# First block of a fused two-block transformer kernel: GpSimd arithmetic moved to VectorE and ScalarE, and the memory input split 512 columns at a time

## The chip, the cores and the metric

The kernel runs on one core of one Trainium2 chip. The metric is the device time of one execution in microseconds; lower is better. The core's engines work side by side, each through its own queue in order: TensorE (PE in the rows, PEld for its weight loads), VectorE (DVE), ScalarE (ACT), GpSimd (POOL) and SyncE (SP), which issues the DMAs. Engines wait for one another by semaphores.

## The reference, cut to what matters

256 tokens of width 1024 pass through a first block (depth 1) and a second one (two layers). The change is in the first part of the first block and in a softmax helper that all attentions share.

```python
# first_block, one layer
xn = rmsnorm(h, norm_mix_g[l])
proj = xn @ w_in[l]
q, k, v, u, y = jnp.split(proj, [...], axis=-1)          # 512 columns each
q = rope(q...); k = rope(k...)                            # 8 heads of 64
attn = dilated_mixture_attention(q, k, v)
uc = centred_depthwise_conv(u, conv_w[l], conv_b[l])      # 4 taps
rec = bidirectional_rglru(uc, ...) * jax.nn.gelu(y)
h = h + jnp.concatenate([attn, rec], axis=-1) @ w_out[l]
h = h + memory_cross_attention(rmsnorm(h, ...), rmsnorm(memf, norm_mem_g[l]), ...)
hid = jnp.square(jax.nn.relu(rmsnorm(h, ...) @ w_mlp_in[l]))
h = h + hid @ w_mlp_out[l]

# bidirectional_rglru
r = sigmoid(gate_a(u)); i = sigmoid(gate_x(u))
log_a = -RG_C * r * softplus(-lam)
a = exp(log_a)
b = sqrt(-expm1(2.0 * log_a)) * (i * u)
h_f = scan(a[0], b[0]);  h_b = reverse scan(a[1], b[1]);  return h_f + h_b
```

## The kernel before

Activations are kept with features on the 128 partitions and the 256 tokens along the free dimension. Every weight comes from one stream `W` in blocks of 8 tiles of 128x128, in the order in which they are used. A block is copied in by SyncE (`w`), rounded to a high part by ScalarE (`whi`, line 366) and its remainder taken as a low part (`wlo`, line 368): on VectorE, but on GpSimd for the blocks 6, 9, 12, 15 and 18 (`POOL`). A product of a weight tile with an activation tile is then three matmuls: high by high, high by low, low by high (lines 392 to 394, or 633 to 635 where the weights are the moving side). There are four buffers each of `whi` and `wlo`, so the split of block n waits until TensorE is done with block n-4. I number blocks from 0: u has 0 to 3, q 4 to 7, k 8 to 11, v 12 to 15, y 16 to 19, the memory keys 20 to 23, the output projection 24 to 31. The matmuls of these products (`pl`) I call filler, since small work of the mixers is put between them.

Around them run, as generators: `rglru` (conv `uc`, gates `tr` and `ti`, `e` the exponential, `s` the square root, scans, sum of the two directions), `attention` (8 heads; each head has scores `sc`, maximum on VectorE, exponential `p` on ScalarE, scaling by `rd` in `times`, transposes `ptp`, their copy `pts`, product with the values `po`), `mem_prep` (squares and split of the memory input into `mh` and `ml`), and the rotary products in `c_rope`. `times` is also used by the cross attention and, in the second block's layers, by the two softmax mixers `diff` and `mla`.

The order on each engine is not the order of the code: the build places instructions by a model of their times, with priorities that `urgent` and `norm_later` raise. What stands in that order is therefore a fixed fact of each program.

Of the kernel before, what the change touches and what calls it, by code (L numbers as in the profile page):

```python
# [9 lines left out]
F32 = mybir.dt.float32  # L10
# [4 lines left out]
AF = mybir.ActivationFunctionType  # L15
# [12 lines left out]
NL, NX = 3, 4  # L28
NW = 5
SB = 8  # L30
POOL = range(6, 20, 3)
WARM = 36
G4, H2 = 16, 12
A0, A1 = 2, 4
# [249 lines left out]
class Kern:  # L284
# [71 lines left out]
    def _split(self):  # L356
        t0, size = self.parts[self.ns]
        b, o = divmod(t0, TB)
        while self.nd < min(b + self.depth, self.nblk):
            self._dma()  # L360
        w = self.blk_dma[b][:, o * 128:(o + size) * 128]
        if o + size == TB:
            self.blk_dma.pop(b)
        hi = self.wp.tile([128, SB * 128], F32R, name="whi", tag="whi", bufs=4)[:, :size * 128]
        lo = self.wp.tile([128, SB * 128], F32R, name="wlo", tag="wlo", bufs=4)[:, :size * 128]
        self.nc.scalar.activation(hi, w, AF.Copy)  # L366
        eng = self.nc.gpsimd if t0 // TB in POOL else self.nc.vector
        eng.tensor_tensor(lo, w, hi.bitcast(F32), op=OP.subtract)  # L368
        self.blk_split[self.ns] = (hi, lo)
        self.ns += 1  # L370

# [151 lines left out]
class Body(Kern):  # L523
# [166 lines left out]

    def times(self, p, r):

        self.nc.gpsimd.tensor_tensor(p, p, r.rearrange("p (q o) -> p q o", o=1).to_broadcast([128, 2, T]),  # L693
                                     op=OP.mult)

    def transpose_p(self, p):

# [23 lines left out]
    def setup(self):  # L721
        nc, a, cst = self.nc, self.a, self.cst
        self.h = cst.tile([128, KD, T], F32, name="h")
        self.pt = cst.tile([128, a["P"].shape[1]], F32, name="pt")
        self.ct = cst.tile([128, a["C"].shape[1]], F32, name="ct")
        self.mk = cst.tile([128, 896], U8, name="mk")
        self.xx = cst.tile([128, KD, 2, T], F32R, name="xx")
        self.xh, self.xl = self.xx[:, :, 0], self.xx[:, :, 1]

        z = cst.tile([128, 128], BF16, name="warm")  # L730
        nc.vector.memset(z, 0.0)
        wp = self.psl("warm")
        for _ in range(WARM):
            nc.tensor.matmul(wp[:, :128], z, z, start=True, stop=True)

        nc.scalar.activation(self.small("first", 1), z[:, :1], AF.Square)
        nc.sync.dma_start(self.pt, a["P"])
        for _ in range(32 // TB):
            self._dma()
        self.pos = cst.tile([128, 64], I32, name="pos")  # L740
        p = a["pos"]
        nc.gpsimd.dma_start(self.pos, bass.AP(tensor=p.tensor, offset=p.offset, ap=[[64, 4], [0, 32], [1, 64]]))
        nc.sync.dma_start(self.ct, a["C"])
        self.mhalf = cst.tile([128, 16], F32, name="mhalf")
        nc.gpsimd.memset(self.mhalf, -0.5)

    def setup_late(self):
        nc, a, cst = self.nc, self.a, self.cst
# [178 lines left out]
    def block1(self):  # L927
# [15 lines left out]
        rm = {}  # L943

        def mem_prep():
            nm = Norm(self)
            for j in range(4):
                m = self.mem[j // 2]
                o = 2 * (j % 2)
                sq = self.square(m[:, o:o + 2])  # L950
                for c in range(2):
                    k = 2 * j + c
                    self.split(mh[k // 4][:, k % 4], ml[k // 4][:, k % 4], m[:, k % 4],
                               scale=self.G("norm_mem_g")[:, k:k + 1])
                yield
                nm.add(sq)
            yield
            rm["r"] = self.rpow("mr", nm.sums(), 2, 1.0 / D, EPS)
            yield
            rm["b"] = nm.spread(rm["r"], "mb")  # L960
            yield
# [10 lines left out]
        def c_rope(dst):  # L972
            def f(k, ps, n):
                qe = self.h2("qe")
                V.tensor_tensor(qe, ps, self.bT(r1["b"]), op=OP.mult)
                sw = self.swap(qe, 32)

                def later():
                    V.tensor_tensor(qe, qe, self.bT(self.rope[:, 0]), op=OP.mult)
                    nc.gpsimd.tensor_tensor(sw, sw, self.bT(self.rope[:, 1]), op=OP.mult)  # L980
                    V.tensor_tensor(dst[:, k:k + 2], qe, sw, op=OP.add)
                self.defer(later)
            return f
# [4 lines left out]
        def rglru():  # L988
            yield
            cw, cb = self.G("conv_w"), self.G("conv_b")  # L990
            for c in range(4):
                nc.gpsimd.tensor_scalar(uc[:, c], ut[:, c], cw[:, 4 * c + 2:4 * c + 3], cb[:, c:c + 1],
                                        op0=OP.mult, op1=OP.add)
                for k in (0, 1, 3):
                    lo, hi = max(0, 2 - k), T - max(0, k - 2)
                    o = uc[:, c, lo:hi]
                    V.scalar_tensor_tensor(o, ut[:, c, lo + k - 2:hi + k - 2],
                                           cw[:, 4 * c + k:4 * c + k + 1], o, op0=OP.mult, op1=OP.add)
                if c % 2:
                    yield  # L1000
            pre = []
            for z in range(2):
                tr, ti = self.g4("tr"), self.g4("ti")
                for j in range(2):
                    pa = self.ps("pga").rearrange("p (c t) -> p c t", c=2)
                    px = self.ps("pgx").rearrange("p (c t) -> p c t", c=2)
                    for c in range(2):
                        k = 2 * j + c
                        nc.tensor.matmul(pa[:, c], self.gb[0][:, z * 4 + k], uc[:, k], start=True, stop=True)
                        nc.tensor.matmul(px[:, c], self.gb[1][:, z * 4 + k], uc[:, k], start=True, stop=True)  # L1010
                    for c in range(2):
                        k = 2 * j + c
                        i = z * 4 + k
                        nc.scalar.activation(tr[:, k], pa[:, c], AF.Tanh, bias=self.hb[:, i:i + 1], scale=0.5)
                        nc.scalar.activation(ti[:, k], px[:, c], AF.Tanh, bias=self.hb[:, 8 + i:9 + i], scale=0.5)
                    yield

                V.scalar_tensor_tensor(tr, tr, 1.0, self.sp2[:, 4 * z:4 * z + 4].rearrange("p (k o) -> p k o", o=1)
                                       .to_broadcast([128, 4, T]), op0=OP.add, op1=OP.mult)
                s, e = self.g4("s"), self.g4("e")  # L1020
                nc.scalar.activation(e, tr, AF.Exp, scale=-2.0)
                last = nc.scalar.activation(s, tr, AF.Tanh)
                V.scalar_tensor_tensor(ti, ti, 1.0, uc, op0=OP.add, op1=OP.mult)
                yield

                nc.gpsimd.tensor_scalar(e, e, 0.5, 0.5, op0=OP.mult, op1=OP.add)
                V.scalar_tensor_tensor(tr, s, 1.0, e, op0=OP.add, op1=OP.mult)
                V.scalar_tensor_tensor(e, tr, 2.0, e, op0=OP.subtract, op1=OP.mult)
                nc.gpsimd.tensor_tensor(ti, ti, e, op=OP.mult)
                pre.append((tr, ti, s, e))  # L1030
                yield

            with self.tc.issue_after(last.ins):
                for tr, ti, s, e in pre:
                    nc.scalar.activation(s, s, AF.Sqrt)
            yield
            for z, (tr, ti, s, e) in enumerate(pre):
                V.tensor_tensor(ti, ti, s, op=OP.mult)
                nc.gpsimd.tensor_scalar(e, e, -2.0, -1.0, op0=OP.mult, op1=OP.add)
                for k in range(4):  # L1040
                    if z == 0:
                        V.tensor_tensor_scan(tr[:, k], e[:, k], ti[:, k], 0.0, OP.mult, OP.subtract)
                    else:
                        V.tensor_tensor_scan(tr[:, k, ::-1], e[:, k, ::-1], ti[:, k, ::-1], 0.0,
                                             OP.mult, OP.subtract)
                yield
            self.hh = pre[0][0]
            nc.gpsimd.tensor_tensor(self.hh, pre[0][0], pre[1][0], op=OP.add)

        rg = urgent(self.tc, rglru(), HR)  # L1050

# [9 lines left out]
        def c_y(k, ps, n):  # L1061
# [1 line left out]
            y = yt[:, k:k + 2]  # L1063
            V.tensor_tensor(y, ps, self.bT(r1["b"]), op=OP.mult)
            w = self.h2("yw")
            nc.scalar.activation(w, y, AF.Square)
            nc.gpsimd.tensor_scalar(w, w, 0.044715, 1.0, op0=OP.mult, op1=OP.add)
            nc.gpsimd.tensor_tensor(w, w, y, op=OP.mult)
            nc.scalar.activation(w, w, AF.Tanh, scale=math.sqrt(2 / math.pi))
            V.scalar_tensor_tensor(y, w, 1.0, y, op0=OP.add, op1=OP.mult)  # L1070

# [739 lines left out]
```

## Time and profile before

| | |
|---|---|
| median of 3 runs | 1342.47 us (1341.91 to 1343.61) |
| the profiled execution, its own time | 1340.12 us |
| span of its instructions | 1338.3 us |
| mean granted TensorE clock | 0.982 |
| TensorE busy | 95% of the span |
| VectorE, ScalarE, GpSimd busy | 73%, 50%, 19% |

A busy share is an average over stages: most of the span is long matrix products in which TensorE never stops, while the first 137 us are the mixed stage that the change touches. So that stage has to be read by itself, by who waits for whom in it.

### The profile page before, as it was taken

The numbers are of one execution on the slowest core, as the hardware profiler recorded it, in microseconds if no ns is written. First come the engines' busy times: TensorE is split into PE (matmuls) and PEld (weight loads), VectorE is DVE, ScalarE is ACT, GpSimd is POOL, SyncE is SP. The second block draws the span as 40 slices with busy tenths as digits, with TensorE's granted clock in tenths as the row PEclk, the third lists the DMA queues.
The fourth block names the chain that finished last, engine by engine and source line by source line (L and its number), as shares of the span: only waits on it lengthen the run. The fifth ranks groups of instructions, "written<-read, shape, count | busy, mean of one in ns | idle before, by whom it ended". The sixth has DMA issues, their size and how long they took to land. (4 is left out here: it accounts for less than half of the span.)

```text
span 1338.3 us, 21771 instructions
## 1 busy us (share of the span) xinstructions
PE 1277.3 (95%) x8514; PEld 1159.8 (87%) x8514; DVE 974.8 (73%) x1398; ACT 667.4 (50%) x1018; POOL 258.7 (19%) x209
## 2 busy tenths in 40 slices
PE   7969999999989889999999999998899999999998
PEld 7957978888879888899988888898788999888886
DVE  6998548775568997656777776689966667777754
ACT  5556446554444226444555554442363545555542
POOL 8764111000012331222010000024212220100000
PEclk9989999999999999999999999998998999999999
DMA  8532445565564353245555566544431355555552
GB/s 275 172 118 96 141 126 166 190 190 189 194 205 150 118 181 95 89 143 179 179 184 190 189 200 223 168 146 127 159 125 64 129 186 175 179 191 191 191 187 68
DMA packets 68599, 216.45 MB, mean 162 GB/s; under 512 B 10376, under 2 KB 16008, under 8 KB 68496
## 3 DMA queue, kind: packets, MB, share of 16 engines
q1 hardware_dynamic: 68448, 215.02, 49.0%
q8 instruction: 67, 1.10, 0.4%
q14 instruction: 36, 0.29, 0.1%
q0 software_dynamic: 48, 0.03, 0.0%
HBM read 208.73 MB, written 1.05 MB: 157 GB/s over the span
## 5 line engine op out<-in xcount | busy, mean ns | idle before, releaser
L368 DVE TENSOR_TENSOR wlo<-w,whi 128x1024 fp32r<-128x1024 f32 (+1 forms) x381 | 490.0, 1289 | 236.1 <-ACT whi L366 233.7
L366 ACT ACTIVATE whi<-w 128x1024 fp32r<-128x1024 f32 (+1 forms) x386 | 404.2, 1051 | 475.5 <-PE pl L393 156.7
L589 PE MATMUL pw<-xx,whi 128*128 128x512 f32 x960 | 334.5, 392 | 3.0 <-DVE xx L403 2.9
L394 PE MATMUL pl<-xx,wlo 128*128 128x256 f32 x912 | 265.0, 291 | 13.7 <-DVE wlo L368 8.0
L392 PE MATMUL pl<-xx,whi 128*128 128x256 f32 x912 | 265.1, 291 | 7.3 <-ACT xx L399 3.3
L590 PE MATMUL pw<-xx,wlo 128*128 128x256 f32 x960 | 269.1, 281 | 0.1
L393 PE MATMUL pl<-xx,whi 128*128 128x256 f32 x912 | 265.4, 291 | 0.7 <-DVE xx L403 0.6
L589 PEld LDWEIGHTS pw<-xx,whi 128*128 128x128 f32 x960 | 179.5, 187 | 43.3 <-DVE xx L403 4.3
L394 PEld LDWEIGHTS pl<-xx,wlo 128*128 128x128 f32 x912 | 179.4, 197 | 16.4 <-DVE wlo L368 8.8
L392 PEld LDWEIGHTS pl<-xx,whi 128*128 128x128 f32 x912 | 179.2, 197 | 10.9 <-ACT xx L399 3.7
L590 PEld LDWEIGHTS pw<-xx,wlo 128*128 128x128 f32 x960 | 181.4, 189 | 0.6 <-DVE wlo L368 0.4
L393 PEld LDWEIGHTS pl<-xx,whi 128*128 128x128 f32 x912 | 179.3, 197 | 2.9 <-DVE xx L403 1.3
L589 PE MATMUL pw<-fw,whi 128*128 128x512 f32 x352 | 124.6, 398 | 1.8 <-DVE rs L603 0.9
L473 POOL TENSOR_TENSOR sq<-sq 128x512 f32<-128x512 f32 x24 | 33.4, 1398 | 474.8 <-ACT sq L457 455.7
L590 PE MATMUL pw<-fw,wlo 128*128 128x256 f32 x352 | 99.0, 281 | 0.8 <-DVE wlo L368 0.8
L589 PE MATMUL pw<-hd,whi 128*128 128x512 f32 x256 | 89.1, 392 | 2.7 <-DVE rs L603 2.7
L589 PEld LDWEIGHTS pw<-fw,whi 128*128 128x128 f32 x352 | 66.1, 188 | 18.5 <-DVE rs L603 1.3
L590 PE MATMUL pw<-hd,wlo 128*128 128x256 f32 x256 | 71.7, 280 | 0.0
L590 PEld LDWEIGHTS pw<-fw,wlo 128*128 128x128 f32 x352 | 66.5, 189 | 1.4 <-DVE wlo L368 1.4
L589 PEld LDWEIGHTS pw<-hd,whi 128*128 128x128 f32 x256 | 47.9, 187 | 13.6 <-DVE rs L603 3.0
L693 POOL TENSOR_TENSOR p<-p,rd 128x512 f32<-128x512 f32 x28 | 33.5, 1198 | 120.4 <-DVE rd L686 57.5
L590 PEld LDWEIGHTS pw<-hd,wlo 128*128 128x128 f32 x256 | 48.4, 189 | 0.0
(433 smaller groups left out, 2146.4 us busy)
## 6 DMA issues: line engine op xcount, KB each, us to landing
w<-in_W_dram SPq DMA_DIRECT2D x378, 512.0 KB, 3.5
w<-in_W_dram SPq DMA_DIRECT2D x8, 256.0 KB, 4.5
sw<-in_S_dram SPq DMA_DIRECT2D x4, 512.0 KB, 5.7
h<-in_xT_dram SPq DMA_DIRECT2D x8, 128.0 KB, 4.1
mem<-in_memT_dram SPq DMA_DIRECT2D x2, 512.0 KB, 6.5
sw<-qe SPq DMA_DIRECT2D x16, 64.0 KB, 2.4
dt<-in_C_dram SPq DMA_DIRECT2D x4, 256.0 KB, 7.4
dqs<-dhi SPq DMA_DIRECT2D x16, 64.0 KB, 3.0
```

What stands on the lines that cost most here:

```text
L366: self.nc.scalar.activation(hi, w, AF.Copy)
L368: eng.tensor_tensor(lo, w, hi.bitcast(F32), op=OP.subtract)
L392: mm(out, wh, xh, start=first, stop=False, skip_group_check=shared)
L393: mm(out, wh, xl, start=False, stop=False, skip_group_check=shared)
L394: mm(out, wl, xh, start=False, stop=last, skip_group_check=shared)
L473: self.eng.tensor_tensor(self.acc, self.acc, sq, op=OP.add)
L589: mm(ps[:, c], wh, x, start=k == 0, stop=False, skip_group_check=True)
L590: mm(ps[:, c, 0], wl, x[:, 0], start=False, stop=k == K - 1, skip_group_check=True)
L693: self.nc.gpsimd.tensor_tensor(p, p, r.rearrange("p (q o) -> p q o", o=1).to_broadcast([128, 2, T]), op=OP.mult)
```

## The change

The low part of every weight block is now taken on VectorE. `times` becomes two ScalarE activations with a scale per partition. In `rglru` the conv's first tap, the two affine steps on `e` go to ScalarE (with constants moved so that `e` is doubled and the square root takes a factor of 1/16), and the product `ti*e` and the final sum go to VectorE. The rotary `sw` product goes to VectorE. In `c_y` two GpSimd steps become one VectorE step. The sums of squares of the memory input go to VectorE. The memory input is scaled in place by ScalarE (eight 256-column activations) and then split with four 512-column pairs instead of eight 256-column ones.

```diff
-        eng = self.nc.gpsimd if t0 // TB in POOL else self.nc.vector
-        eng.tensor_tensor(lo, w, hi.bitcast(F32), op=OP.subtract)
+        self.nc.vector.tensor_tensor(lo, w, hi.bitcast(F32), op=OP.subtract)
...
     def times(self, p, r):
-        self.nc.gpsimd.tensor_tensor(p, p, r.rearrange("p (q o) -> p q o", o=1).to_broadcast([128, 2, T]),
-                                     op=OP.mult)
+        for q in range(2):
+            self.nc.scalar.activation(p[:, q], p[:, q], AF.Copy, scale=r[:, q:q + 1])
...
-            nm = Norm(self)
+            nm = Norm(self, eng=V)
...
-                    self.split(mh[k // 4][:, k % 4], ml[k // 4][:, k % 4], m[:, k % 4],
-                               scale=self.G("norm_mem_g")[:, k:k + 1])
+                    nc.scalar.activation(m[:, k % 4], m[:, k % 4], AF.Copy, scale=self.G("norm_mem_g")[:, k:k + 1])
                 yield
+                self.split(mh[j // 2][:, o:o + 2], ml[j // 2][:, o:o + 2], m[:, o:o + 2])
...
-                    nc.gpsimd.tensor_tensor(sw, sw, self.bT(self.rope[:, 1]), op=OP.mult)
+                    V.tensor_tensor(sw, sw, self.bT(self.rope[:, 1]), op=OP.mult)
...
-                nc.gpsimd.tensor_scalar(uc[:, c], ut[:, c], cw[:, 4 * c + 2:4 * c + 3], cb[:, c:c + 1],
-                                        op0=OP.mult, op1=OP.add)
+                nc.scalar.activation(uc[:, c], ut[:, c], AF.Identity, bias=cb[:, c:c + 1],
+                                     scale=cw[:, 4 * c + 2:4 * c + 3])
...
-                nc.gpsimd.tensor_scalar(e, e, 0.5, 0.5, op0=OP.mult, op1=OP.add)
+                nc.scalar.activation(e, e, AF.Identity, bias=1.0)
                 V.scalar_tensor_tensor(tr, s, 1.0, e, op0=OP.add, op1=OP.mult)
-                V.scalar_tensor_tensor(e, tr, 2.0, e, op0=OP.subtract, op1=OP.mult)
-                nc.gpsimd.tensor_tensor(ti, ti, e, op=OP.mult)
+                V.scalar_tensor_tensor(e, tr, 4.0, e, op0=OP.subtract, op1=OP.mult)
+                V.tensor_tensor(ti, ti, e, op=OP.mult)
...
-                    nc.scalar.activation(s, s, AF.Sqrt)
+                    nc.scalar.activation(s, s, AF.Sqrt, scale=1.0 / 16)
...
-                nc.gpsimd.tensor_scalar(e, e, -2.0, -1.0, op0=OP.mult, op1=OP.add)
+                nc.scalar.activation(e, e, AF.Identity, bias=self.minus, scale=-0.5)
...
-            nc.gpsimd.tensor_tensor(self.hh, pre[0][0], pre[1][0], op=OP.add)
+            V.tensor_tensor(self.hh, pre[0][0], pre[1][0], op=OP.add)
...
-            nc.scalar.activation(w, y, AF.Square)
-            nc.gpsimd.tensor_scalar(w, w, 0.044715, 1.0, op0=OP.mult, op1=OP.add)
-            nc.gpsimd.tensor_tensor(w, w, y, op=OP.mult)
+            nc.scalar.activation(w, y, AF.Square, scale=math.sqrt(0.044715))
+            V.scalar_tensor_tensor(w, w, 1.0, y, op0=OP.add, op1=OP.mult)
```

Since the build places instructions anew, the order changes too. The first place is VectorE's queue at the end of the rotary tables (`rt` is their last step, `l` the small arithmetic of `derived`, `v` the sum for the first norm). Before, the low part of block 6 is not in it, since GpSimd takes it; the next low parts (blocks 7, 8 and 10) stand behind all of the small steps:

```order
L368 TENSOR_TENSOR wlo<-w,whi 128x1024
L795 TENSOR_SCALAR l_220<-l_218 128x8
L870 TENSOR_TENSOR rt_250<-rt_249 128x64
L793 TENSOR_TENSOR l_222<-l_220,l_198 128x8
...
L409 TENSOR_SCALAR v<-ss 128x2
L801 SCALAR_TENSOR_TENSOR sp_238<-l_234,l_236 128x8
L804 TENSOR_SCALAR sp_240<-sp_238 128x8
L806 TENSOR_SCALAR spm_242<-sp_238 128x8
L368 TENSOR_TENSOR wlo<-w,whi 128x1024 x3
L966 TENSOR_TENSOR ut<-plk,n1b 128x512 x2
```

Of the change, in the same place:

```order
L366 TENSOR_TENSOR wlo<-w,whi 128x1024
L793 TENSOR_TENSOR l_228<-l_226,l_200 128x8
L870 TENSOR_TENSOR rt_252<-rt_251 128x64
L366 TENSOR_TENSOR wlo<-w,whi 128x1024
L795 TENSOR_SCALAR l_230<-l_228 128x8
...
L407 TENSOR_SCALAR v<-ss 128x2
L801 SCALAR_TENSOR_TENSOR sp_240<-l_236,l_238 128x8
L366 TENSOR_TENSOR wlo<-w,whi 128x1024
L804 TENSOR_SCALAR sp_242<-sp_240 128x8
L806 TENSOR_SCALAR spm_244<-sp_240 128x8
L366 TENSOR_TENSOR wlo<-w,whi 128x1024 x2
```

The low part of block 6 stands right behind the rotary step `rt`, and that of block 7 ahead of two of the small steps. (On ScalarE the high part of block 6, which stood ahead of the sine step `sc` before, now stands behind it.)

The second place is ScalarE's queue at the first heads of the attention (`p,den` is a head's exponential, `sb` its scores with their bias). Before:

```order
L683 ACT_TABLE_LOAD
L683 ACTIVATE p,den<-sb,nm 128x256 x2
L366 ACTIVATE whi<-w 128x1024
L1035 ACT_TABLE_LOAD
L1035 ACTIVATE s<-s 128x1024
L490 ACTIVATE mbb<-mbp 128x256
L366 ACTIVATE whi<-w 128x1024
L683 ACT_TABLE_LOAD
L683 ACTIVATE p,den<-sb,nm 128x256 x2
L366 ACTIVATE whi<-w 128x1024 x2
```

Of the change:

```order
L365 ACTIVATE whi<-w 128x1024 x2
L681 ACT_TABLE_LOAD
L681 ACTIVATE p,den<-sb,nm 128x256 x2
L365 ACTIVATE whi<-w 128x1024
L1039 ACTIVATE e<-e,minus 128x1024
L365 ACTIVATE whi<-w 128x1024
L692 ACTIVATE p<-p,rd 128x256 x2
L365 ACTIVATE whi<-w 128x1024
L681 ACTIVATE p,den<-sb,nm 128x256 x2
L365 ACTIVATE whi<-w 128x1024
L692 ACTIVATE p<-p,rd 128x256 x2
L365 ACTIVATE whi<-w 128x1024
```

Both square roots now stand ahead of the first exponential, and the high parts of the blocks up to 27 stand between the first three heads.

The third place is TensorE's queue in the middle of the attention. Before, each head's matmuls stand between fillers (here of the memory keys, `mh` and `ml`):

```order
L701 MATMUL ptp<-ct,p 128x128 x4
L1094 MATMUL sc<-kr,qr 128x256 x2
L394 MATMUL pl<-mh_305,wlo 128x256
L1105 MATMUL po<-pts,vv 64x256 x2
L392 MATMUL pl<-mh_305,whi 128x256
L393 MATMUL pl<-ml_307,whi 128x256
L394 MATMUL pl<-mh_305,wlo 128x256
```

Of the change, the last filler, then a head, and the last heads:

```order
L392 MATMUL pl<-mh_307,wlo 128x256
L699 MATMUL ptp<-ct,p 128x128
L1093 MATMUL sc<-kr,qr 128x256 x2
L699 MATMUL ptp<-ct,p 128x128 x3
L1104 MATMUL po<-pts,vv 64x256 x2
...
L699 MATMUL ptp<-ct,p 128x128 x8
L390 MATMUL pl<-mxh_488,whi 128x256
L1104 MATMUL po<-pts,vv 64x256 x2
L391 MATMUL pl<-mxl_490,whi 128x256
```

The fillers of q, k, v, y and the memory keys, 432 matmuls, are now all issued before the second head's transposes, 402 of them before the first head's. Before, 303 stood ahead of the first head's transposes and 129 between the heads. The first 12 matmuls of the output projection stand among the last heads in both.

## Rows read from the trace of the kernel before

**Rows 1.** The page's part 1: busy us (share of the span) and instructions.
```profile
PE   1277.3 (95%) x8514; PEld 1159.8 (87%) x8514; DVE 974.8 (73%) x1398; ACT 667.4 (50%) x1018; POOL 258.7 (19%) x209
```

**Rows 2.** Windows: length, busy time (count) of PE, PEld, DVE, ACT, POOL, clock, DMA.
```profile
26.00:31.70 5.70, 0.03 (x1) 0.03 (x1) 4.02 (x4) 3.44 (x5) 5.37 (x8) 0.91 0.50 137
72.00:81.30 9.30, 2.60 (x12) 1.84 (x11) 9.30 (x7) 5.81 (x7) 7.80 (x4) 0.85 0.25 78
96.60:102.30 5.70, 5.70 (x20) 4.53 (x21) 5.39 (x4) 1.35 (x2) 4.16 (x2) 0.50 0.45 154
137.00:167.00 30.00, 29.14 (x240) 28.73 (x241) 19.23 (x24) 15.31 (x23) 5.23 (x4) 1.00 0.44 141
```

**Rows 3.** Waits of TensorE from 5 to 137 us: total, times, longest.
```profile
PE pl L394 <- POOL wlo L368: 5.7, 1, 5.7
PE pl L394 <- DVE wlo L368: 5.5, 1, 5.5
PE ptp L701 <- POOL p L693: 4.6, 1, 4.6
PE pl L634 <- POOL wlo L368: 1.2, 1, 1.2
```

**Rows 4.** Timeline at the first stall: start, duration, engine, line, idle before it.
```profile
27.23 0.26 ACT L881 ACTIVATE sc<-rt 128x64 f32<-128x64 f32 x1 [4.87 <-POOL rt L824]
27.56 0.23 DVE L870 TENSOR_TENSOR rt<-rt 128x64 f32<-128x64 f32 x1 [6.29 <-POOL rt L824]
...
29.27 2.35 POOL L368 TENSOR_TENSOR wlo<-w,whi 128x1024 fp32r<-128x1024 f32 x1
31.67 0.58 PE L394 MATMUL pl<-xx,wlo 128*128 128x256 f32 x1 [5.69 <-POOL wlo L368]
```

**Rows 5.** Timeline of VectorE and GpSimd ahead of the second stall, and two quiet steps.
```profile
47.64 0.48 DVE L997 SCALAR_TENSOR_TENSOR uc<-ut,pt,uc 128x255 f32<-128x255 f32 x1
74.49 1.21 DVE L1018 SCALAR_TENSOR_TENSOR tr<-tr,sp 128x1024 f32<-128x1024 f32 x1
74.65 3.27 POOL L1029 TENSOR_TENSOR ti<-ti,e 128x1024 f32<-128x1024 f32 x1 [1.50 <-DVE e L1028]
75.63 3.38 DVE L1023 SCALAR_TENSOR_TENSOR ti<-ti,uc 128x1024 f32<-128x1024 f32 x1
```

**Rows 6.** Groups of VectorE by form, 31 to 137 us: count, busy, mean ns.
```profile
L368 DVE TENSOR_TENSOR wlo<-w,whi 128x1024 fp32r<-128x1024 f32 x17 | 29.9, 1762 | 1.0 <-PE pl L394 0.5 <-ACT whi L366 0.5
L403 DVE SCALAR_TENSOR_TENSOR ml<-mem,pt,mh 128x256 fp32r<-128x256 f32 x8 | 8.2, 1053 | 0.0
L981 DVE TENSOR_TENSOR kr<-qe,sw 128x512 f32<-128x512 f32 x2 | 3.6, 1776 | 0.0
L981 DVE TENSOR_TENSOR qr<-qe,sw 128x512 f32<-128x512 f32 x2 | 1.4, 680 | 0.0
```

**Rows 7.** The same view, 234 to 300 us, where GpSimd does nothing.
```profile
L368 DVE TENSOR_TENSOR wlo<-w,whi 128x1024 fp32r<-128x1024 f32 x24 | 29.4, 1225 | 13.9 <-ACT whi L366 13.9
```

**Rows 8.** Timeline of one head and of the marks on TensorE.
```profile
67.76 0.58 PE L436 MATMUL ss<-ct,sq 128*128 128x1 f32 x4
116.40 0.60 PE L701 MATMUL ptp<-ct,p 128*128 128x128 f32 x4
116.93 1.13 PE L1094 MATMUL sc<-kr,qr 64*128 64x256 f32 x4
118.54 1.08 PE L1105 MATMUL po<-pts,vv 128*64 128x256 f32 x4
136.83 0.51 PE L392 MATMUL pl<-mxh,whi 128*128 128x256 f32 x2 [0.69 <-ACT mxh L399]
```

**Rows 9.** Groups of ScalarE by form, 31 to 137 us.
```profile
L366 ACT ACTIVATE whi<-w 128x1024 fp32r<-128x1024 f32 x19 | 19.7, 1058 | 7.0 <-POOL wlo L368 5.6 <-ACT whi L366 0.7 <-PE pl L393 0.7
L683 ACT ACTIVATE p<-sb,nm 128x256 f32<-128x256 f32 x16 | 8.0, 501 | 6.3 <-DVE nm L677 6.1
L704 ACT ACTIVATE pts<-ptp 128x512 f32<-128x512 f32 x8 | 4.6, 580 | 0.9 <-PE ptp L701 0.9
```

More of the change, by code (lines that the diff above doesn't have):

```diff
@@ L30 @@
 SB = 8
-POOL = range(6, 20, 3)
 WARM = 36
@@ L745, in setup @@
         nc.gpsimd.memset(self.mhalf, -0.5)
+        self.minus = cst.tile([128, 1], F32, name="minus")
+        nc.gpsimd.memset(self.minus, -1.0)
     def setup_late(self):
```

## Prediction

> **What bounds the kernel now.** I read the page's part 1 first. TensorE is busy 95% of the span and GpSimd 19% [rows 1], so only a stall of TensorE can be worth anything. The windows show where one is: from 137 to 167 us TensorE issues 240 matmuls in 29.1 us, 0.12 us each, with nothing to win, while from 26 to 31.7 us it does nothing and from 72 to 81.3 us it is busy 2.6 of 9.3 us [rows 2]. The list of waits names four stalls before 137 us: 5.7 us on a low part that GpSimd makes, 5.5 us on a low part that VectorE makes, 4.6 us on a head's scaling on GpSimd, 1.2 us on a GpSimd low part [rows 3]. That is 17.0 us. [...]
>
> Why is VectorE late for its stall? It never idles there (9.30 of 9.30 us busy [rows 2]), and one of its instructions takes 3.38 us whose like takes 1.21 us next to it; it ends 1.1 us after a GpSimd product of 3.27 us, having started inside it [rows 5]. The groups tell the same: in the mixed stage a low part takes 1762 ns [rows 6], and 1225 ns where GpSimd is quiet [rows 7]. By such pairs 17 low parts lose 9.1 us, eight `ml` at 1053 ns lose 4.6 us against a quiet step of their width at 0.48 us [rows 5, 6], two `kr` lose 2.2 us against `qr` at 680 ns [rows 6]. That is 15.9 us of VectorE's time in these 106 us that I put down to waiting inside its own instructions, for GpSimd; smaller groups, which I leave out, should add to it.
>
> **The change, part by part.** VectorE gets work: five low parts at 1.225 us (6.1 us), two products `ti*e` and the sum of the directions at the same size (3.7), four rotary products at 0.68 (2.7), the sums of squares (four at about 0.6) and two steps in `c_y` (1.4). The wider memory split takes back about 1.0. Together 15 us [rows 5 to 7]. It loses some 16 us of stretching, so its load stays about what it was. What decides is the order of its work.
>
> ScalarE gets some 17 us: 16 scalings of 256 columns at about 0.5 us, the four affine steps on `e` at about 1.06, and the conv and memory steps [rows 9]. I price a scaling like the exponential of that size, which has the nearest form; half a copy `pts` of 512 columns, 0.29, is the lower bound and 0.5 the upper. ScalarE is busy 50% [rows 1], so I cost most of that at nothing; it counts where a head waits for it, below.
>
> First stall. In the new order the high part of block 6 stands behind the sine step `sc`, which starts at 27.23 us and frees ScalarE at 27.5. So that high part ends near 28.5 and the low part, right behind the rotary step on VectorE, near 29.8. TensorE restarts there and not at 31.67 [rows 4, 7, 9]: 1.9 us gained. The stall is still about 3.8 us, so I leave what the clock does behind it as it is.
>
> The other two stalls on low parts. I added up VectorE's new queue from the first norm's products (about 34.6 us) with quiet durations: the low part of block 15 lands near 67.2 us, and TensorE asks for it near 68. Those of blocks 16 to 23 land 2 to 5 us ahead of TensorE. Both stalls go, 6.7 us. Block 15 is the tightest place: if VectorE is 2 us later there, 1 us of stall comes back.
>
> Stall on the scaling. TensorE no longer meets the first head's transposes behind 303 fillers, but behind 402, so the scaling is there first. This stall goes, with its half-rate stretch: 4.6 and 2.9 us.
>
> What is late next. TensorE passes the sums of the memory norm at 67.76 us now [rows 8]; with 1.9 us gained, at about 66. Behind them stand 209 fillers, 17 of them of 512 columns at about double time: 27 us. With four heads' scores (1.13 each) and one head's transposes (0.60) [rows 8] it has no filler left near 99 us. There the tail begins: eight value products, seven transposes, four scores and 12 matmuls, 18.8 us of TensorE's time [rows 8], with nothing to hide a wait. ScalarE has more to do in the same tail: a high part (1.06), six exponential pairs (1.0), eight copies (0.58), six pairs of scalings (0.9), and five or six `yw` and `mx` steps of about 0.6 [rows 9]: 20 to 21 us. So it sets the pace. After its last copy come the last product and one rounding, 1.7 us. The output projection then starts near 122 us, where it starts at 136.8 now [rows 8]: 14.8 us gained, the sum of all the above net of some 4 us of new waiting in the tail. I take off 1.3 us for one stretch at half clock in a tail in which TensorE idles a sixth of the time.
>
> From there to the end the same work follows. In the cross attention and the two layers, `times` moves 20 more pairs of scalings (four in the cross attention, sixteen in the layers) to ScalarE: half a microsecond less latency each at best, but behind whatever ScalarE's queue holds. I take 1 us gained, with bounds of 4 gained and 3 lost.
>
> The sum: 1340.1 - 14.8 + 1.3 - 1.0 = 1325.6 us against the profiled execution, which ran 2.4 us under the median of the runs shown; so 1328.0 us.
>
> [...] GpSimd's product of a whole low part takes 2.35 us [rows 4] and VectorE's 1.225 [rows 7]. [...]
>
> **The rivals.**
> - The tail runs at the lower clock. [...] For it: a stretch at 0.50 stands behind a stall now, and around the longer two stalls the clock is 0.85 [rows 2]. Against it: the new waits are short, about 0.6 us a head. [...] Chance 0.20.
> - More is gained: the tail is bound by TensorE alone (projection at 118) and the later attentions give their 4 us. That is 18.8 + 4 less: 1319.7 us. For it: a scaling may cost 0.29 us. Chance 0.20.
> - Slower. The long VectorE instructions are not stretched by GpSimd but by something that stays. Then VectorE, which has no idle moment around its stall now [rows 2], gets 15 us more. It decides from the point at which less than about 15 us of stretching goes: what is missing makes low parts late, each microsecond about one of TensorE's, once the 3 to 5 us that VectorE idles elsewhere in the stage are used up. If nothing goes, the stage ends 10 to 12 us later, about 1353. Against it: the stretched step of 3.38 us ends just behind a GpSimd step, and the same low part is short where GpSimd is quiet [rows 5 to 7]. Chance 0.06.
> - The change does nothing: the tail gives back what the stalls gave, within 2.7 us of the median. Chance 0.04.
> - The forecast, 1322 to 1334: chance 0.50.
>
> **How the numbers follow.** A measurement of this kernel tells 0.2%, 2.7 us, from no change. The first rival's upper end lies inside that bound, a fifth of its chance; so same is 0.06 with most of that from the clock and the do-nothing case, slower 0.06, faster 0.88. The range from 1316 to 1340 holds the forecast, most of the better case and most of the clock case.
>
> **What would show it.** In the changed profile: TensorE restarts near 30 us; no wait on `wlo` over 1 us between 35 and 95; `wlo` near 1225 ns and `kr` near 680 ns in the mixed stage; GpSimd almost idle from 35 to 140; all fillers done near 99 and the projection's main run from about 122. The prediction is wrong if VectorE's groups stay long, if the clock shows 0.50 through the tail, or if a wait on ScalarE's scaling of over 1.5 us stands before every head. It is also wrong if the second block's layers lose what the first block gained.

## The result, and the profile after

The changed kernel takes 1326.17 us (median of four runs, 1322.45 to 1329.48), the kernel before, run beside it, 1343.04 us (1341.91 to 1345.81). The ratio is 0.9871, with a 95% interval of 0.9839 to 0.9902. The profiled execution took 1322.45 us with a span of 1320.6, so it lies 3.7 us under its median, and that of before 2.9 us under its own: the two traces are 17.7 us apart, the medians 16.9.

The page's part 1, of the changed kernel, beside [rows 1]:

```profile
PE 1269.5 (96%) x8514; PEld 1153.2 (87%) x8514; DVE 957.9 (73%) x1412; ACT 694.7 (53%) x1084; POOL 177.4 (13%) x154
```

The windows, of the changed kernel, over the stretches of [rows 2], then over its attention's tail and the mixed stage (length, busy time and count of PE, PEld, DVE, ACT, POOL, clock, DMA share, GB/s):

```profile
26.00:31.70 5.70, 2.21 (x15) 1.80 (x15) 2.66 (x10) 3.77 (x6) 3.98 (x10) 0.97 0.36 114
31.70:37.50 5.80, 5.80 (x39) 5.63 (x38) 5.80 (x9) 3.14 (x6) 2.90 (x2) 0.73 0.98 275
72.00:81.30 9.30, 7.24 (x59) 6.55 (x59) 9.30 (x14) 5.35 (x7) 4.25 (x1) 1.00 0.68 206
96.60:102.30 5.70, 4.86 (x35) 4.07 (x34) 4.66 (x12) 4.58 (x10) 0.00 (x0) 1.00 0.39 129
99.70:120.60 20.90, 18.13 (x88) 10.46 (x87) 13.37 (x44) 19.42 (x53) 0.00 (x0) 1.00 0.15 51
31.00:137.00 106.00, 100.91 (x676) 87.68 (x675) 91.00 (x164) 81.79 (x150) 10.45 (x4) 0.98 0.53 155
```

The same view of the kernel before over the mixed stage:

```profile
31.00:137.00 106.00, 93.11 (x547) 77.74 (x548) 95.88 (x143) 60.52 (x112) 65.50 (x39) 0.91 0.42 133
```

In these 106 us GpSimd's busy time falls from 65.5 to 10.5 us, ScalarE's rises by 21 us, and VectorE's falls by 4.9 us although it runs 21 instructions more. TensorE issues 129 matmuls more in the same time, and its mean clock is 0.98 instead of 0.91.

Two more windows of the kernel before, behind its first and its second long stall:

```profile
31.70:37.50 5.80, 5.80 (x27) 5.80 (x28) 5.61 (x11) 0.89 (x1) 4.75 (x3) 0.50 1.10 272
81.30:92.00 10.70, 10.70 (x71) 9.98 (x71) 10.70 (x14) 5.05 (x9) 6.79 (x4) 0.81 0.46 149
```

From these and from 96.6 to 102.3 us [rows 2] one can estimate what the clock alone is worth, since TensorE is busy throughout in all three: 5.8 us at 0.50, 10.7 at 0.81 and 5.7 at 0.50. If the work goes with the clock, they lack 2.9, 2.0 and 2.9 us of full-rate work, 7.8 in sum. The changed kernel lacks 1.6 us (5.8 at 0.73), and its clock is 1.00 from 37.5 to 137 us. That makes some 6 us. The matmuls of 128x256 show a little less: they start 0.21 us apart in the first of these stretches and 0.12 us from 137 to 167 us, so 0.44 of the time is lost there and not 0.50, and by that it is 5.4 us. So some 5 to 6 us of the gain come from the clock, by estimate.

What VectorE gained stands in its groups by form, 31 to 122 us, of the changed kernel:

```profile
L366 DVE TENSOR_TENSOR wlo<-w,whi 128x1024 fp32r<-128x1024 f32 x21 | 26.0, 1248 | 1.8 <-ACT whi L365 1.8
...
L981 DVE TENSOR_TENSOR kr<-qe,sw 128x512 f32<-128x512 f32 x2 | 1.4, 679 | 0.0
```

A low part takes 1248 ns instead of 1762, `kr` 679 instead of 1776 [rows 6], both now about as in quiet stretches (1225 [rows 7], and 680 for `qr` [rows 6]). Over all groups, each instruction set against the short end of its form's durations in these traces, VectorE's instructions from 31 to 137 us were 30 us too long in sum before and are 1.5 us too long in the changed kernel.

The waits of TensorE from 5 to 137 us, of the changed kernel (total, times, longest), against [rows 3]:

```profile
PE pl L390 <- ACT whi L365: 2.7, 1, 2.7
PE mbp L427 <- POOL mr L409: 2.1, 1, 2.1
PE po L1104 <- ACT pts L702: 1.5, 2, 0.8
PE pl L392 <- DVE wlo L366: 1.5, 2, 0.8
```

The four stalls of before are gone or shortened; the sum of all waits in the list falls from 18.6 to 10.5 us. The longest of the new ones: TensorE stands 2.06 us before the spread of the memory norm (`mbp`), because its reciprocal root `mr`, two elements a partition on GpSimd, takes 5.62 us. The timeline of the changed kernel at its first stall, at that wait, and at the end of the tail (start, duration, engine):

```profile
27.93 0.26 ACT L881 ACTIVATE sc<-rt 128x64 f32<-128x64 f32 x1 [6.00 <-POOL rt L824]
...
29.19 0.39 PE L390 MATMUL pl<-xx,whi 128*128 128x256 f32 x1 [2.74 <-ACT whi L365]
...
30.45 0.39 PE L392 MATMUL pl<-xx,wlo 128*128 128x256 f32 x1 [0.76 <-DVE wlo L366]
...
70.63 5.62 POOL L409 TENSOR_TENSOR mr<-v,mhalf 128x2 f32<-128x2 f32 x1 [36.03 <-DVE v L407]
...
75.02 0.68 DVE L981 TENSOR_TENSOR kr<-qe,sw 128x512 f32<-128x512 f32 x1
...
76.31 0.32 PE L427 MATMUL mbp<-ct,mr 128*128 128x128 f32 x1 [2.06 <-POOL mr L409]
...
99.38 0.28 PE L392 MATMUL pl<-mh,wlo 128*128 128x256 f32 x1
...
120.63 0.50 PE L390 MATMUL pl<-mxh,whi 128*128 128x256 f32 x2 [0.69 <-ACT mxh L397]
```

The first stall is 3.5 us in two pieces instead of 5.69 [rows 4]. The last filler is issued at 99.38, and the output projection's main run starts at 120.63, 16.2 us ahead of its 136.83 [rows 8]. That is nearly all of the 17.7 us between the traces. Setting the n-th matmul of a weight tile in one trace against the n-th in the other, the lead is 16.2 us before the cross attention, 14.7 behind it, and 17.3 at the end.

### The profile page after: what moved, and what is told of

Read it like the earlier page. It is cut to its first block, busy times and chain, and to the rows that moved or that the text cites. A ratio compares the mean times of both kernels' runs of the same rounds, so it can differ in the third digit from the quotient of the medians.

```text
span 1320.6 us, 21734 instructions
## 1 busy us (share of the span) xinstructions
PE 1269.5 (96%) x8514; PEld 1153.2 (87%) x8514; DVE 957.9 (73%) x1412; ACT 694.7 (53%) x1084; POOL 177.4 (13%) x154
## 5 line engine op out<-in xcount | busy, mean ns | idle before, releaser
L471 POOL TENSOR_TENSOR sq<-sq 128x512 f32<-128x512 f32 x21 | 29.4, 1405 | 536.7 <-ACT sq L455 440.0
L587 PEld LDWEIGHTS pw<-hd,whi 128*128 128x128 f32 x256 | 48.7, 190 | 13.9 <-DVE rs L601 3.0
L1391 POOL TENSOR_TENSOR qz<-hq,ct 128x1024 f32<-128x1024 f32 x14 | 36.2, 2588 | 53.8 <-DVE hq L1410 34.1
```

The costliest lines, as they stand in the source:

```text
L471: self.eng.tensor_tensor(self.acc, self.acc, sq, op=OP.add)
L587: mm(ps[:, c], wh, x, start=k == 0, stop=False, skip_group_check=True)
L1391: nc.gpsimd.tensor_tensor(qz.rearrange("p h (n b) -> p (h n) b", b=2 * B), hq.rearrange("p h (n b) -> p (h n) b", b=2 * B), zm, op=OP.mult)
```

## The experiments

My theory: GpSimd's work cost time by its own latency and, more, by making VectorE's instructions on two memory inputs longer; taken away, both go. The first rival: only the faster engine counts. The second: the new order of instructions brings the gain. Each run was timed against the kernel before on the same chip; the ratios are against it, and the changed kernel's is 0.9871.

**The parts alone.** First the low parts of the five blocks moved to VectorE, in the kernel before:

```diff
-        eng = self.nc.gpsimd if t0 // TB in POOL else self.nc.vector
-        eng.tensor_tensor(lo, w, hi.bitcast(F32), op=OP.subtract)
+        self.nc.vector.tensor_tensor(lo, w, hi.bitcast(F32), op=OP.subtract)
```

> The kernel before with only the low parts of all weight blocks on VectorE. Theory (GpSimd's work makes low parts late in two ways, by its own latency and by stretching VectorE): the two stalls on GpSimd's low parts go or shrink to 4 us, and part of the stall on VectorE's, but the other GpSimd products stay and still stretch VectorE, so 1334 to 1339 us against 1342.5. Rival (only the faster product counts, 2.35 against 1.225 us): 1340 to 1341 us, and the low parts on VectorE stay at about 1.76 us.

Measured: 1333.37 us, ratio 0.9919 (0.9904 to 0.9935). That is a little more gain than my range and far from the rival's 1340. VectorE's low parts fell to 1457 ns in the mixed stage, though there were more of them.

Then only `times`, in the kernel before:

```diff
-        self.nc.gpsimd.tensor_tensor(p, p, r.rearrange("p (q o) -> p q o", o=1).to_broadcast([128, 2, T]),
-                                     op=OP.mult)
+        for q in range(2):
+            self.nc.scalar.activation(p[:, q], p[:, q], AF.Copy, scale=r[:, q:q + 1])
```

> The kernel before with only the softmax scalings on ScalarE, in all attentions. Theory: the stall of 4.6 us on the first head's scaling and its half-rate stretch of 2.9 us mostly go, the stalls on low parts stay, ScalarE's extra work costs nothing while fillers are left: 1335 to 1341 us. Rival (the scalings sit in ScalarE's queue behind high parts and make every head wait, in the layers too): 1343 to 1348 us.

Measured: 1344.78 us, ratio 1.0008 (0.9994 to 1.0021), so nothing is gained. My expectation failed, and the time lies in the rival's range. TensorE's two longest waits in it, 5 to 137 us:

```profile
PE pl L394 <- POOL wlo L368: 6.2, 1, 6.2
PE ptp L701 <- ACT p L694: 5.5, 3, 2.4
```

The wait on the scaling did not go; it became a wait on ScalarE, longer in sum. Another engine for the scaling does not by itself remove that stall.

Third, the gate, rotary and memory arithmetic alone: the changed kernel with the last two diffs taken back.

> The changed kernel with the low parts of five blocks and the scalings given back to GpSimd: only the gate, rotary and memory arithmetic is moved. Theory: most of the stretching of VectorE goes, since the long GpSimd products stood there, so the low part of block 15 is no longer 5.5 us late; the stall on the first low part and on the scaling stay: 1332 to 1338 us, low parts in the mixed stage at 1.3 to 1.5 us. Rival (stretching is not GpSimd's doing): VectorE only has more to do, 1343 to 1353 us.

Measured: 1331.44 us, ratio 0.9909 (0.9893 to 0.9925), just under my range, low parts at 1346 ns. The two parts that work alone bring 9.5 and 11.4 us and together 16.9, so in part they remove the same loss; that it is the lateness of VectorE is argued.

**The contention by itself.** The changed kernel with 18 products on GpSimd in place, on the masks' staging tile behind its last use. On TensorE, VectorE, ScalarE and SyncE the order of instructions is the same, one for one:

```diff
         nc.gpsimd.tensor_copy(self.mk, mf[:, :n])
+        [nc.gpsimd.tensor_tensor(mf[:, :448], mf[:, :448], mf[:, 448:896], op=OP.mult) for _ in range(18)]
```

> The changed kernel with 18 products of 448 columns added on GpSimd alone from about 35 us on, on data that nothing needs; every other engine's order is the same. Theory (GpSimd's two-input work stretches VectorE's): before, GpSimd's 75 us in 33 to 133 us went with 27 us of stretching, so some 25 us of such work stretch VectorE by 8 to 10 us, low parts take over 1.5 us in that stretch, and TensorE waits for low parts again: 4 to 8 us slower than the changed kernel, 1330 to 1334 us. Rival (the gain came from the new order and GpSimd's own latency): nothing waits for these products, so no change, 1325 to 1327 us, low parts at 1.25 us.

Measured: 1339.45 us, ratio 0.9972 (0.9961 to 0.9982). Work that nothing waits for costs 13.3 us. The rival on the order falls with it, since the order is that of the changed kernel and does not keep the gain. The 13.3 us are not contention's share of the 16.9, since I chose the dose: these products make VectorE's instructions 14 us longer (below), half of what the change had removed, all in one place. Groups of VectorE in this run, 31 to 62 us:

```profile
L997 DVE SCALAR_TENSOR_TENSOR uc<-ut,pt,uc 128x255 f32<-128x255 f32 x8 | 10.4, 1351 | 0.0
L366 DVE TENSOR_TENSOR wlo<-w,whi 128x1024 fp32r<-128x1024 f32 x6 | 9.3, 1560 | 0.0
L997 DVE SCALAR_TENSOR_TENSOR uc<-ut,pt,uc 128x254 f32<-128x254 f32 x4 | 4.8, 1216 | 0.0
L884 DVE COPY sel<-ct 128x128 f32<-128x128 f32 x4 | 2.6, 698 | 0.0
L471 DVE TENSOR_TENSOR sq<-sq 128x512 f32<-128x512 f32 x2 | 2.3, 1147 | 0.0
L975 DVE TENSOR_TENSOR qe<-pl,n1b 128x512 f32<-128x512 f32 x3 | 2.0, 677 | 0.0
```

The same groups of the changed kernel, in the stretch to 54 us, in which it does the same steps of the conv:

```profile
L366 DVE TENSOR_TENSOR wlo<-w,whi 128x1024 fp32r<-128x1024 f32 x7 | 9.1, 1319 | 0.0
L997 DVE SCALAR_TENSOR_TENSOR uc<-ut,pt,uc 128x255 f32<-128x255 f32 x8 | 3.4, 471 | 0.0
L471 DVE TENSOR_TENSOR sq<-sq 128x512 f32<-128x512 f32 x3 | 2.0, 677 | 0.0
L975 DVE TENSOR_TENSOR qe<-pl,n1b 128x512 f32<-128x512 f32 x3 | 2.0, 677 | 0.0
L997 DVE SCALAR_TENSOR_TENSOR uc<-ut,pt,uc 128x254 f32<-128x254 f32 x4 | 1.8, 470 | 0.0
...
L884 DVE COPY sel<-ct 128x128 f32<-128x128 f32 x4 | 0.6, 216 | 0.0
```

The conv's steps go from 470 to 1351 and 1216 ns, 10 us in sum (10.4 and 4.8 against 3.4 and 1.8); six low parts lose 1.4, the copies `sel` 2.0 and two squares `sq` 0.9. That is some 14 us over 18 products, 0.8 us each. And `qe`, one of whose inputs is TensorE's result in PSUM, stays at 677 ns, though two of the three ran beside products. So the steps that got longer have two memory inputs, or are the copies `sel`, which have one and go from 216 to 698 ns; what makes the difference is not shown.

My 4 to 8 us were too few: I had 8 to 10 us of stretching instead of 14 (worked out from 75 us of GpSimd's work before, where the trace has 64.6 from 33 to 133 us), and I counted on fillers. The next matmul in TensorE's queue reads the conv's `uc` (the list of waits has 7.2 us ahead of it and names no releaser), and a window of this run shows what followed:

```profile
50.00:60.00 10.00, 5.37 (x16) 4.60 (x17) 10.00 (x8) 0.00 (x0) 9.14 (x7) 0.52 0.15 52
```

ScalarE, which works on what TensorE makes there, did nothing, and the clock was at 0.52.

The same with 24 scalings of 896 columns by a constant (one memory input):

```diff
+        [nc.gpsimd.tensor_scalar(mf[:, :896], mf[:, :896], 1.0, None, op0=OP.mult) for _ in range(24)]
```

> The changed kernel with 24 scalings of 896 columns by a constant added on GpSimd alone from about 35 us on (one input from memory, where the run before had products of two), on data that nothing needs; the other engines' order is the same. If only GpSimd's work on two inputs stretches VectorE: the conv's steps on VectorE stay at 0.47 us and the whole at 1325 to 1328 us. If any GpSimd work does: those steps take over 0.9 us, as they did beside the products (1.35 and 1.22 us), and the whole is 1335 to 1341 us.

Measured: 1338.51 us, ratio 0.9970 (0.9955 to 0.9985), as for contention by any GpSimd work; but the conv's steps took 558 and 720 ns, between the two cases. Ten of the scalings ran from 34 to 66 us; then GpSimd waited 10.2 us for VectorE's `v` and made `mr`; the other fourteen ran from 81 to 121 us, beside the attention's heads, and the tail took 29.2 us instead of 21.2. (TensorE's order is not quite the changed kernel's here: the build put the spread of the memory norm later.) So two stretches were mixed, and I repeated it with nine (`range(9)`). The rival that I set against it rests on a misreading, since `mr` did not wait for the scalings:

> As the run with 24 scalings added on GpSimd, but with 9, so that they end near 61 us and nothing that is needed stands behind them on GpSimd; the other engines' order is that of the changed kernel. Theory (each GpSimd step, on one input too, makes one VectorE step about 0.7 us longer): 9 times 0.7 is 6 us more in VectorE's queue, of which 2 to 6 us reach TensorE: 1328 to 1333 us. Rival (the 24 scalings cost time because the memory norm's root stood behind them on GpSimd): 1325 to 1327 us.

Measured: 1329.30 us, ratio 0.9903 (0.9887 to 0.9919): as the theory had it. That is 3.1 us behind the changed kernel, but the two intervals overlap, so the size is not firm. In the trace its last filler is issued at 103.9 us, where the changed kernel has 99.4, and the tail is as long. The added steps, and VectorE beside them:

```profile
L758 POOL TENSOR_SCALAR mf<-mf 128x896 f32<-128x896 f32 x9 | 27.5, 3053 | 0.8
```

```profile
43.59 1.22 DVE L366 TENSOR_TENSOR wlo<-w,whi 128x1024 fp32r<-128x1024 f32 x1
44.72 1.15 DVE L997 SCALAR_TENSOR_TENSOR uc<-ut,pt,uc 128x255 f32<-128x255 f32 x1
45.79 0.68 DVE L471 TENSOR_TENSOR sq<-sq 128x512 f32<-128x512 f32 x1
46.39 1.26 DVE L997 SCALAR_TENSOR_TENSOR uc<-ut,pt,uc 128x255 f32<-128x255 f32 x3
```

GpSimd's step takes 3.05 us, and in the timeline one step of VectorE in several is longer by 0.7 us (1.15 for 0.47), the others not at all. Set step against step of the changed kernel, whose order this run has, eight of VectorE's are longer, by 4.7 us in sum: 0.5 us for each scaling. So work on one input, too, made VectorE's steps longer here. But none of those shown waits for a whole step of GpSimd: GpSimd's steps follow one another with 0.8 us of idle time in all, and still five of the six steps of VectorE shown ran at their quiet length beside them, all on two memory inputs, while the sixth is longer by 0.7 us, less than a quarter of a step of 3.05 us.

**Giving a part back.** The changed kernel with the low parts of five blocks on GpSimd again:

```diff
-        self.nc.vector.tensor_tensor(lo, w, hi.bitcast(F32), op=OP.subtract)
+        eng = self.nc.gpsimd if t0 // TB in POOL else self.nc.vector
+        eng.tensor_tensor(lo, w, hi.bitcast(F32), op=OP.subtract)
```

> The changed kernel with the low parts of the blocks 6, 9, 12, 15 and 18 back on GpSimd, all else as in it. Theory: the first stall is longer by about 2 us, each of the five takes 2.5 to 4.5 us and stretches VectorE's work beside it by 1 to 2 us: 1330 to 1335 us. Rival (VectorE is the fuller engine now and is glad to be rid of 6 us of work): 1322 to 1326 us.

Measured: 1336.30 us, ratio 0.9946 (0.9924 to 0.9968), just above my range: about 10 us of the gain are gone. Those five, and the longest waits of TensorE, in this run:

```profile
L368 POOL TENSOR_TENSOR wlo<-w,whi 128x1024 fp32r<-128x1024 f32 x5 | 15.0, 3009 | 25.8 <-ACT whi L366 15.6 <-DMA sw<-qe 10.1
```

```profile
PE sc L1095 <- DVE kr L983: 5.0, 1, 5.0
PE pl L394 <- POOL wlo L368: 2.7, 1, 2.7
```

VectorE is late again, now with `kr`, although it has 6 us less to do; one of its steps ahead of `kr`, the product `ti`, takes 3.39 us beside a low part on GpSimd, where it took 1.21. The rival is refuted. The build placed this run anew, so some of the 10 us can be order.

The changed kernel with the old `times` in all attentions (the diff of the run with only `times`, taken back):

> The changed kernel with all softmax scalings back on GpSimd, one product of 512 columns each. Theory (ScalarE sets the pace of the attention's tail, 20 to 21 us against TensorE's 18.8): the tail gets 1 to 3 us shorter, and with the later attentions the whole is 1320 to 1324 us. Rival (a scaling on GpSimd is late as it was, about 3 us beside VectorE's work, and stretches VectorE in the tail): a wait on the scaling of 2 us or more comes back, 1326 to 1332 us.

Measured: 1325.96 us, ratio 0.9867 (0.9846 to 0.9888): no difference. No wait on the scaling comes back, so the rival falls; but the tail did not get shorter either:

```profile
99.80:121.40 21.60, 17.97 (x86) 10.49 (x85) 14.56 (x45) 14.67 (x41) 6.24 (x6) 1.00 0.14 50
```

ScalarE is busy 14.7 us of the tail here and 19.4 us in the changed kernel, and the tail takes 21.6 us and 20.9. (The heads' order differs in this run from 93 us on.)

The old `times` only behind the first block's attention:

```diff
 def times(self, p, r):
-        for q in range(2):
+        if self.act_times:
+            for q in range(2):
...
+        else:
+            self.nc.gpsimd.tensor_tensor(p, p, r.rearrange("p (q o) -> p q o", o=1).to_broadcast([128, 2, T]),
+                                         op=OP.mult)
...
+        self.act_times = False
         r2 = self.norm_later(n2, "n2")
```

> The changed kernel with the scalings of the cross attention and of the two layers back on GpSimd; those of the first block's heads stay on ScalarE and that block's order is the same up to the cross attention. Theory (the later scalings cost on ScalarE: the cross attention of the run with only the scalings moved ended 1.4 us later): 1321 to 1325 us. Rival (they gain half a microsecond of latency each, as the forecast's bound had it): 1327 to 1330 us.

Measured: 1327.40 us, ratio 0.9886 (0.9866 to 0.9907): in the rival's range, and not told apart from the changed kernel. Up to the cross attention its order is the changed kernel's, one for one, and still its trace has the projection's main run at 122.94 us, 2.3 us later, with a mean clock of 0.91 from 72 to 90 us where the changed kernel has 1.00. So much do two executions of one order differ; the lead of 16.2 us above is that of one execution.

The traces show one place where the later scalings matter. TensorE's waits around the cross attention, of the changed kernel, then of this run:

```profile
PE ptp L699 <- ACT p L692: 1.9, 2, 1.7
PE pl L390 <- ACT ch L397: 1.3, 2, 0.7
PE po L1186 <- ACT pts L702: 0.7, 1, 0.7
```

```profile
PE pl L391 <- ACT ch L398: 1.5, 2, 0.8
PE ptp L704 <- POOL p L696: 1.3, 2, 1.1
```

With the scalings on ScalarE the cross attention ends 1.4 us later, in every run that has them there. What they do in the two layers drowns in what profiled executions differ by there: behind the cross attention the changed kernel's gained 2.6 us, and this run's, with the engine of before, lost 6.0.

**Towards a faster one.** In the changed kernel ScalarE and VectorE wait 6.0 us each for GpSimd's rotary chain (until 27.93 and 28.26 us), with the split of block 6 queued behind. I queued the last VectorE step of the tables and the sine steps behind later splits:

```diff
-        nc.vector.tensor_tensor(ab, a, na, op=OP.max)
...
+        with self.tc.issue_after(self.split_ins[1]):
+            nc.vector.tensor_tensor(ab, a, na, op=OP.max)
+        with self.tc.issue_after(self.split_ins[0]):
+            nc.scalar.activation(self.rope_sc[:, 0], ab, AF.Sin, bias=hp, scale=-1.0)
+            nc.scalar.activation(self.rope_sc[:, 1], a, AF.Sin)
```

> The changed kernel with the last VectorE step of the rotary tables and both sine steps queued behind the splits of later weight blocks. In the changed kernel ScalarE is idle 6.0 us and VectorE 6.0 us before these steps, with the split of block 6 behind them, and TensorE waits 2.74 and 0.76 us. Theory (that stall is order alone: an in-order queue behind a step that waits for GpSimd's chain): it goes, and the half-rate clock behind it, 2 to 5 us faster than the changed kernel: 1321 to 1324 us. Rival (TensorE then waits for the norm's reciprocal root, which stands behind the same GpSimd chain): the same as the changed kernel, 1325 to 1327 us.

Measured: 1334.06 us, ratio 0.9933 (0.9917 to 0.9948), slower than both cases. The stall moved to the first norm's root `n1r`, as the rival had it, and a second one followed, since a high part stood behind that norm on ScalarE:

```profile
31.88 0.72 POOL L410 TENSOR_TENSOR n1r<-v,mhalf 128x2 f32<-128x2 f32 x1
...
32.65 0.43 PE L428 MATMUL n1p<-ct,n1r 128*128 128x128 f32 x2 [2.62 <-POOL n1r L410]
...
33.12 0.38 ACT L489 ACTIVATE n1b<-n1p 128x256 f32<-128x256 f32 x1 [7.72 <-PE n1p L428]
...
35.38 1.04 ACT L365 ACTIVATE whi<-w 128x1024 fp32r<-128x1024 f32 x1
...
39.91 0.53 PE L393 MATMUL pl<-xx,wlo 128*128 128x256 f32 x1 [2.47 <-DVE wlo L366]
```

Added to that, more steps between `mr` and its use:

```diff
             rm["r"] = self.rpow("mr", nm.sums(), 2, 1.0 / D, EPS)
-            yield
+            for _ in range(4):
+                yield
```

> The run before with three more steps of the schedule between the memory norm's reciprocal root on GpSimd (128x2 elements, 5.62 us beside a full VectorE in the changed kernel) and TensorE's use of it. Theory (TensorE's wait of 2.06 us for it goes, since other matmuls stand ahead): 1.5 to 2.5 us faster than the run before. Rival (the wait only moves to the keys' eviction, or the new order costs as much): the same as the run before within 1 us.

Measured: 1328.40 us, ratio 0.9892 (0.9875 to 0.9908). The wait on `mr` is gone, and the run is 5.7 us faster than the one before it, more than the 2.7 us that `mr` had cost there and more than I expected; the new order changed other waits too.

Last, the end of the rotary chain (in `tail`) and the cast of the masks queued behind `n1r` too:

```diff
+        with self.tc.issue_after(self.rpow_ins):
+            ab, a, na = tail()
...
+        with self.tc.issue_after(self.rpow_ins):
+            nc.gpsimd.tensor_copy(self.mk, mf[:, :n])
```

> The run with both moves (sine steps behind later splits, three more steps ahead of the use of the memory norm's root), and now the last part of the rotary chain on GpSimd and the cast of the masks queued behind the first norm's reciprocal root, which is ready to start at about 25 us and stood behind that chain until 31.9. Theory (TensorE's wait of 2.5 us for it, and the wait of 2.5 us for the low part that stood behind its eviction, are order on GpSimd): both go, 3 to 6 us faster than the run with both moves, 1322 to 1325 us, and no slower than the changed kernel. Rival (the memsets and the rotary steps still ahead of the root keep it until after 29 us, or the wait moves to the rotary tables): within 2 us of the run with both moves, 1326 to 1330 us.

Measured: 1328.67 us, ratio 0.9894 (0.9877 to 0.9910): the time is the rival's, its reason is not. `n1r` now starts at 25.4 us, not after 29, and TensorE no longer waits for it; but TensorE's first stall is still there, on a low part and not on the rotary tables:

```profile
PE pl L393 <- DVE wlo L366: 3.5, 2, 2.8
```

No run here is measurably faster than the changed kernel.

## Why the prediction was right, step by step

- **Stretching.** Right, and shown by the run with 18 products that nothing needs: same order, 13.3 us lost. I put the lost time at some 16 us, from three groups, and VectorE's load at about what it was; over all forms the loss was 30 us, nearly twice that, and the load fell by 4.9 us. By the engines' speeds alone (2.35 against 1.225 us for a low part) the rival of the first run had 1340 to 1341; moving the low parts alone gave 1333.37, so they are not the whole. GpSimd's own steps on one input vary, too: in the kernel before, an affine step `e` of 1024 columns took 1.04 us at 83.74 us, beside a VectorE that was busy throughout, and one of the same form 1.90 us at 98.94 us, while the added scalings of 896 columns took 3.05 us (nine) and 2.89 (24) in the mean. Why is open.
- **First stall.** Right: 2.2 us gained for the 1.9 of the sum, TensorE on the low part again at 30.45 for 29.8. I had left the clock behind it as it was; it went from 0.50 to 0.73 in 31.7 to 37.5 us.
- **The other two stalls on low parts.** Right: no low part is waited for over 1 us between 35 and 95. Not foreseen: the 2.06 us on `mr`. I had looked at what GpSimd does to VectorE, not at what a VectorE without pauses does to the one small step left on GpSimd.
- **Stall on the scaling.** It went, and its half-rate stretch with it (the clock is 1.00 from 96.6 to 102.3 us). No run shows the 2.9 us that the sum has for that stretch: they are an estimate from the trace before, which has a clock of 0.50 there over 5.7 us. The engine of the scaling is not what did it: moved alone it gains nothing, put back it costs nothing. That fits the forecast's reason, the place in the order and VectorE being in time, but no run kept the scaling's old place in the order with all else changed, so this is argued.
- **The tail.** The times were right (fillers out at 99.4 for 99, main run at 120.6 for 122), one reason was wrong: I wrote that ScalarE sets the pace. In the changed kernel TensorE is busy 18.13 of 20.9 us and its waits there are 0.84, 0.41 and twice 0.69 us; with 5 us less on ScalarE, and the scaling back on GpSimd, the tail was no shorter (21.6 us). By the trace, TensorE's own work and the waits at the tail's two ends set it, with 2.8 us of waiting where I had 4; no run tests that.
- **The clock.** No run shows the 1.3 us that I took off for the tail, nor a tail at half clock: the clock stayed at 1.00 from 99.7 to 120.6 us. Outside the tail I had it too small: I counted the stretch behind the scaling, 2.9 us, and left out those behind the other two long stalls, and the clock gave back some 5 to 6 us by the estimate above. (I also wrote that it is 0.85 around the longer two stalls; that is the second, and around the first it is 0.91.)
- **The sum of the parts.** It does not come out as I wrote. The four gains are 1.9, 6.7, 4.6 and 2.9, 16.1 us, and net of 4 us of new waiting that is 12.1, not 14.8. The 14.8 came from the times of the tail alone, and 2.7 us of it stood under no part; the clock that I had left out, some 2.5 to 3 us by the same estimate, is about as large.
- **The later attentions.** Mis-sized in the cross attention: 1.4 us lost where the sum had 1 us gained in all; for the layers it stays open. That the two traces gain 1.1 us between the projection and the end, near my 1, is luck: it is 1.4 lost and 2.6 gained, and the 2.6 are less than what two executions differ by there. The wider memory split was not run apart.

Summed up to the output projection the forecast had 14.8 less 1.3, 13.5 us, and the traces show 16.2 (13.9 in the run with the same order up to there). The total was 14.5 us under the median then known, and 16.9 were measured. The mechanism and the path were right; that the total is so near also rests on a stretching and a clock put too small beside losses that were not in the sum.

## What to carry to other kernels

Count GpSimd's work against VectorE's: 18 GpSimd steps that nothing waits for cost 13.3 us here, where VectorE was the late engine, and the added steps made VectorE's longer, by 0.8 us in the mean for a product and 0.5 us for a scaling. Look for it in the groups by form: one shape with two means, one of them long only where GpSimd is busy (a low part 1762 and 1225 ns here), is a better sign than any busy share. And an engine that looks full in a stretch is not thereby its limit: ScalarE was busy 19.4 of 20.9 us of the tail, and with 14.7 the tail took 21.6. Take work off it and see whether the stretch gets shorter.

## What I had not expected of the hardware

GpSimd's steps, too, were longer beside VectorE's here. The root `mr` on 128x2 elements took 5.62 us beside a VectorE that ran two-input steps without a pause, 1.67 us in the kernel before, and the like of it 0.72 us where VectorE was idle (`n1r` above, at 31.88). It ended at 76.25 us, 0.56 us after `kr`, the last of five such steps without a gap. In the run with the low parts given back, two such steps stood in a row, and `mr` took 2.74 us and ended 0.56 us after the second. So in these two runs the small step lasted as long as the row, and 0.56 us more. And the smallest step on GpSimd was the one that TensorE waited for, 2.06 us in the changed kernel.
